# Embedding product of the short tile: both parts of its operand side by side

## The chip, the cores and the metric

The kernel runs on one core of one Trainium2 chip. The metric is the device time of one execution in microseconds, as the median of several runs. The profile is taken on one further execution, whose span (first to last instruction) is a little shorter than its device time.

## The reference, cut to what matters

One layer of a streaming encoder trunk is computed for a prompt of 2048 rows and a sample of 32 rows, with 1024 channels. The last step of the layer adds a gated embedding; a final norm closes it:

```python
    h = h + jnp.concatenate([yA, yB], axis=-1) @ w_out
    gate = jax.nn.sigmoid(rmsnorm(h, g_ple) @ w_ple_gate)
    h = h + (p @ w_ple) * gate
    ...
    return rmsnorm(h, g_final)
```

`p` has 256 channels and `w_ple` is 256 x 1024. The product `p @ w_ple` for the 32 sample rows is what the change touches.

## The kernel before

**Precision.** The products' operands are of type fp32r, to which fp32 is rounded. Each operand is therefore split into an upper part (ACT casts it) and a lower part (DVE subtracts the upper from the original, `split`, L77), and a product is the sum of three: upper x upper, upper x lower, lower x upper.

**Rows.** The 2080 rows are 17 tiles: 16 of 128 rows, and tile 16 with the 32 sample rows, the short tile. `tiles[i]` gives first row and number of rows.

**Stages.** The first stage computes the input projection and the mixers in groups of 416 columns (L572) and, as side work, transposes the embedding inputs `p`, splits them and stores them to `pp_d` (`turn_p`, L1155 to L1193), one record of 128 x 512 for each tile: upper and lower part, two chunks of 128 channels, up to 128 rows. The second stage multiplies with `w_out` in pairs of tiles by a scheme of seven half-size products instead of eight (`seven`, L204, products at L161). Then come the embedding products, then the gate stage, in pairs again.

**The embedding product** of a tile (`embed`, L119) loads the record `pps` from `pp_d` (`load_pps`, L113, on POOL's queue here), multiplies it with the two parts of `w_ple` (`wq`) for each half of the columns, `nh`, into one bank of PSUM (`e`), has ACT copy the bank to `eout` (L141) and stores `eout` to `e_d`, from where the gate stage loads it (`e`). One half of the columns takes two chunks times three combinations, six products, whatever the number of rows:

```python
    def embed_product(ps, pps, wp, cs, n=P):
        for k in range(2):
            for q, (a, b) in enumerate(((0, 0), (0, 1), (1, 0))):
                nc.tensor.matmul(ps[:n], pps[:, a, k, :n], wp[k][b][:, cs], ...)
```

Tiles 3 to 14 and 16 are computed this way before the gate stage, tiles 14 and 16 last. Tiles 0 to 2 were done in the first stage, and tile 15 is done inside the last pair (`last_pair`, L1495).

**The gate stage** begins with the short tile (`plain`, L269, whose products are `packed`, L258). There both parts of the rows lie beside each other already: one product with 64 stationary columns (upper and lower part, L264) and one with 32 (L267) take the place of three, the sums of the lower part stand in rows 32 to 63 of the bank, and DVE adds them (`short_ops`, L1477). Then eight pairs of tiles follow. `prep_g` (L1581) makes a pair's operands while the pair before is computed: DVE transposes one tile of `hn` (L1446), ACT copies the other to `ho` (L1433) for eight transposes on PE (`pth`, L1435), and DVE forms sums (`g_fS`, L1592) and the parts of seven operands (L78, L81). A pair's seven products need, in order, the operands 11, 12, S2, S1, S3, S4 and 22. Their sums leave PSUM by ACT copies (`c_g`, L1455) and DVE additions (L1463); a sigmoid on ACT (L1464), a multiplication and an addition on DVE (L1466, L1467) and the final norm follow (`done_g`: row sums on ACT at L91, 1/sqrt on POOL at L70 and L74, scaling on DVE at L1474, and the store on POOL's queue).

**The order.** The kernel is written in Tile: the framework's scheduler sets the order of the instructions on each engine when the program is built, by estimates of its own, except where the kernel pins it. Each engine then runs its instructions strictly in that order, and DMAs stand in the order of the engine that issues them (SP, POOL or ACT). A changed instruction can so change the order of others that come later.

Of the kernel before, what the change touches and what calls it, by code (L numbers as in the profile page):

```python
# [9 lines left out]
F32 = mybir.dt.float32  # L10
F32R = mybir.dt.float32r
AF = mybir.ActivationFunctionType
ALU = mybir.AluOpType
PSUM = bass.MemoryType.PSUM

P = 128
# [6 lines left out]
PLE = 256  # L23
# [11 lines left out]
def trunk(ctx, tc, x_p, x_s, c_conv, c_pool, p_p, p_s, g_mix, w_in, conv_w, conv_b, pool_w,  # L35
          pool_scale, w_out, g_ple, w_gate, w_ple, g_fin, y_p, y_s, sc_p, sp_p, sc_s, sp_s):
    nc = tc.nc
# [9 lines left out]
    pp_d = tc.dram_tile([NT, P, 2 * PLE], F32, name="pp_d")  # L47
# [5 lines left out]
    def bank(name):  # L53
        return ps_m.tile([P, 512], F32, tag="mm", name=name)
# [22 lines left out]
    def split(hi, lo, src, eng=nc.vector, later=False):  # L77
        ins = nc.scalar.copy(hi, src)  # L78
        if later:
            tc.keep_in_program_order(ins)  # L80
        eng.tensor_tensor(lo, src, hi.bitcast(F32), op=ALU.subtract)  # L81
        return ins
# [14 lines left out]
    tiles = [(i * P, P) for i in range(SEQ // P)] + [(SEQ, DEC)]  # L97
# [1 line left out]
    def rows_of(pr, sa, r, n):  # L99
        return pr[r:r + n] if r < SEQ else sa  # L100

    def embed_product(ps, pps, wp, cs, n=P):
        for k in range(2):
            for q, (a, b) in enumerate(((0, 0), (0, 1), (1, 0))):
                nc.tensor.matmul(ps[:n], pps[:, a, k, :n], wp[k][b][:, cs], start=k + q == 0, stop=k == 1 and q == 2)  # L105


    def load_ple(t, k):
# [2 lines left out]
            nc.sync.dma_start(t[q * 32:q * 32 + 32], w_ple[r:r + 32])  # L111

    def load_pps(t, i, queue):  # L113
        n = tiles[i][1]
        queue.dma_start(t.rearrange("p a k n -> p (a k) n")[:, :, :n].bitcast(F32),
                        pp_d[i].rearrange("p (a n) -> p a n", a=4)[:, :, :n])
        return t

    def embed(todo, wp, ring, queue=nc.sync, loads=nc.sync):  # L119

        got = {}

        def prep(c):
            if c not in got and c < len(todo):
                got[c] = load_pps(ring("pps", todo[c]), todo[c], loads)

        def run(c, last=False):  # L130
            i = todo[c]
            r, n = tiles[i]
            for ahead in range(4):
                prep(c + ahead)
            pps = got[c]
            o = ring("out", i)
            for nh in range(2):
                cs = slice(nh * NH, nh * NH + NH)
                ps = bank(f"e_{i}_{nh}")
                embed_product(ps, pps, wp, cs, n)  # L140
                (nc.vector.tensor_copy if last and nh else nc.scalar.copy)(o[:n, cs], ps[:n])  # L141
            (nc.gpsimd if last else queue).dma_start(e_d[r:r + n], o[:n])

        return prep, run
# [141 lines left out]
    def slot(name):  # L286
        return acts[0].tile([P, SLOT], F32R, tag="hn", name=name)
# [13 lines left out]
    def ring4(t, name):  # L301
        return t.tile([P, D], F32, tag="t", name=name)
# [15 lines left out]
    def load_rows(pool, name, i, pr, sa=None, queue=nc.sync):  # L318
        r, n = tiles[i]
        t = ring4(pool, f"{name}_{i}")  # L320
        queue.dma_start(t[:n], pr[r:r + n] if sa is None else rows_of(pr, sa, r, n))
        return t

    with ExitStack() as s1:
# [152 lines left out]
        def staged(name):  # L477
            return xin.tile([P, KH, 2, P], F32R, tag="t", name=name)
# [676 lines left out]
        def turn_p():  # L1155

            def load(a):
                t = ring4(xin, f"p_{a}")
                for q in range(4):
                    part, cs = t[q * 32:q * 32 + 32], slice(q * 64, q * 64 + 64)  # L1160
                    if a < NT - 1:
                        nc.gpsimd.dma_start(part.rearrange("p (m c) -> p m c", c=64),
                                            p_p[a * P:(a + 4) * P, cs].rearrange("(m p) c -> p m c", p=32))
                    else:
                        nc.gpsimd.dma_start(part[:, :64], p_s[:, cs])
                return t

            rounds = [*range(0, NT - 1, 4), NT - 1]
            t = load(0)
            yield  # L1170
            for a, after in zip(rounds, rounds[1:] + [None]):
                w = D if a < NT - 1 else 64
                nc.vector.transpose(t[:, :w], t[:, :w])
                v = t[:, :w]
                if after is not None:
                    t = load(after)
                yield
                for b in range(0, 4 if w == D else 1, 2):
                    s = staged(f"pps_{a + b}").rearrange("p a h n -> p (a h n)")
                    for c in range(2 if w == D else 1):  # L1180
                        i = a + b + c
                        n = tiles[i][1]
                        o = s[:, c * 2 * PLE:(c + 1) * 2 * PLE].rearrange("p (a k n) -> p a k n", a=2, k=2)[:, :, :, :n]
                        if n == P:
                            src = v[:, (b + c) * PLE:(b + c + 1) * PLE].rearrange("p (g k r) -> p k g r", g=4, k=2)
                            hi, lo = (o[:, h].rearrange("p k (g r) -> p k g r", g=4) for h in range(2))
                        else:
                            src = v.rearrange("p (k r) -> p k r", k=2)
                            hi, lo = o[:, 0], o[:, 1]
                        split(hi, lo, src)  # L1190
                        nc.gpsimd.dma_start(pp_d[i].rearrange("p (a n) -> p a n", a=4)[:, :, :n],
                                            o.rearrange("p a k n -> p (a k) n").bitcast(F32))
                    yield  # L1193

        def at_pace(steps, num, den):
# [12 lines left out]
        for gi, tbs in enumerate(GROUPS):  # L1208
            if gi == 2:

                frames_in.close()
                t = slot("hn_4")
# [37 lines left out]
    with ExitStack() as s2:  # L1250
# [113 lines left out]
        for i in range(0, NT - 1, 2):  # L1364
# [6 lines left out]
            if last:  # L1371
                n = tiles[NT - 1][1]
# [13 lines left out]
        def embedding_chunks(name):  # L1386
            wp = []
            for k in range(2):
                raw = ring4(ya, f"{name}r_{k}")
                load_ple(raw, k)  # L1390
                t = [cmb.tile([P, KH, 2, P], F32R, tag="c", name=f"{name}_{k}_{h}").rearrange("p a b c -> p (a b c)")
                     for h in range(2)]
                split(t[0], t[1], raw)
                wp.append(t)
            return wp

        wp = embedding_chunks("wq")
# [3 lines left out]
        def ring(what, i):  # L1401
            if what == "pps":
                return st.tile([P, 2, 2, P], F32R, tag="t", name=f"pps_{i}")
            if what == "out" and i not in rest_e[-LATE:]:
                return cmb.tile([P, D], F32, tag="c", name=f"eout_{i}")
            return ring4(ya, f"e{what}_{i}")
# [212 lines left out]
        n = tiles[NT - 1][1]  # L1619
# [6 lines left out]
        h, e = (load_rows(*a) for a in ((xh, "h", NT - 1, h_d), (ya, "e", NT - 1, e_d)))  # L1626
        plain("gl", A, W, n, *short_ops(h, e, n))
        done_g(NT - 1, h)
        for i in range(0, NT - 3, 2):
            A = S.pop(i)  # L1630
            h = [load_rows(xh, "h", i + b, h_d) for b in range(2)]
# [34 lines left out]
```

## Time and profile before

| | |
|---|---|
| runs shown | 927.29, 930.17 and 5190.86 us, median 930.17 |
| profiled execution | 929.13 us, span 927.2 us |
| busy in the span | PE 912.1, DVE 719.7, ACT 483.5, POOL 159.6 us |
| matmuls | 4553 |
| granted TensorE clock | 0.998 |

One run is far outside; the others and the profiled execution lie within 2.9 us. The busy time of PE is the time in which a matmul was under way, and consecutive matmuls overlap, so the time that one costs is read from start to start. A row of the timeline has the start in the span, the duration, engine, line, operation, the tile written and the tiles read, the shape and the count; in brackets stands how long the engine had idled before and what ended the idling.

### The profile page before, as it was taken

How to read it: one execution, taken by the hardware profiler on the slowest of the kernel's cores; microseconds unless marked ns; L12 is line 12 of the kernel's file. 1: busy time of each engine (PE TensorE's matmuls, PEld its weight loads, DVE VectorE, ACT ScalarE, POOL GpSimd, SP SyncE). 2: the span in 40 equal slices, each digit the busy share in tenths (PEclk: the TensorE clock that was granted, in tenths of full speed). 3: DMA queues.
4: the chain of work that ended last, by engine and by line, in shares of the span. 5: the costliest groups of instructions: out<-in, count | busy, mean ns of one | idle time of the engine just before them, and what ended most of it. 6: DMA issues, size and time to landing. Idle time of an engine off the chain costs nothing.

```text
span 927.2 us, 13211 instructions
## 1 busy us (share of the span) xinstructions
PE 912.1 (98%) x4553; PEld 826.3 (89%) x4553; DVE 719.7 (78%) x1221; ACT 483.5 (52%) x895; POOL 159.6 (17%) x299
## 2 busy tenths in 40 slices
PE   8999999999999999999999999999999999999996
PEld 6999998999999999999999987888878768888885
DVE  6996989999577869795777678765558658889885
ACT  7743565654345545443544356334336755565563
POOL 3111222121001234110000010111203301111113
PEclk9999999999999999999999999999999999999999
DMA  8357687798936567769655349866787964676663
GB/s 249 98 147 217 168 259 217 230 298 294 410 114 188 173 167 229 187 227 309 184 166 178 122 178 295 266 188 177 227 240 234 377 220 142 227 252 203 200 197 114
DMA packets 135279, 198.58 MB, mean 214 GB/s; under 512 B 12796, under 2 KB 99740, under 8 KB 133933
## 3 DMA queue, kind: packets, MB, share of 16 engines
q1 hardware_dynamic: 115661, 136.65, 47.5%
q0 software_dynamic: 16816, 55.65, 18.8%
q10 hardware_dynamic: 2736, 5.44, 1.8%
q8 instruction: 36, 0.59, 0.3%
q14 instruction: 30, 0.25, 0.1%
HBM read 133.84 MB, written 63.84 MB: 213 GB/s over the span
## 4 chain that ended last, share of the span: by engine, by line
PE 60%; DVE 2%; DMA 2%; issue 1%; ACT 1%; POOL 0%; POOLq 0%; SPq 0%; DVEq 0%; ACTq 0%
PE x_g L161 8%; PE x_o L161 8%; PE z_g L161 4%; PE z_o L161 4%; PE e L105 3%; PE x_zab L572 3%; PE x_ch L572 2%; PE y_g L161 2%; PE x_zbv L572 2%; PE b L572 2%; PE v L572 2%; PE c L572 2%; PE zb L572 2%; PE h L572 2%; PE za L572 2%; PE y_o L161 2%
## 5 line engine op out<-in xcount | busy, mean ns | idle before, releaser
L78 ACT CAST y_S<-y_fS 128x512 fp32r<-128x512 f32 x32 | 19.5, 622 | 40.4 <-PE x_o L161 19.8
L105 PE MATMUL e<-wq,pps 128*128 128x512 f32 (+1 forms) x156 | 36.2, 391 | 0.9 <-DMA pps<-pp_d 0.9
L161 PE MATMUL x_g<-wg_b,g_S 128*128 128x512 f32 x128 | 36.7, 392 | 0.0
L161 PE MATMUL x_o<-wo_b,y_S 128*128 128x512 f32 x128 | 35.8, 391 | 0.0
L105 PEld LDWEIGHTS e<-wq,pps 128*128 128x128 f32 (+1 forms) x156 | 28.2, 182 | 8.2 <-ACT wg_a L78 1.3
L572 PE MATMUL z_ch<-B,w_ch_S 128*128 128x416 f32 x168 | 34.3, 352 | 0.0
L572 PE MATMUL x_zbv<-B,w_zbv_S 128*128 128x416 f32 x168 | 34.2, 352 | 0.0
L572 PE MATMUL z_zbv<-B,w_zbv_S 128*128 128x416 f32 x168 | 34.2, 352 | 0.0
L572 PE MATMUL z_zab<-B,w_zab_S 128*128 128x416 f32 x168 | 34.2, 352 | 0.0
L572 PE MATMUL x_zab<-B,w_zab_S 128*128 128x416 f32 x168 | 34.1, 351 | 0.0
L572 PE MATMUL x_ch<-B,w_ch_S 128*128 128x416 f32 x168 | 34.0, 351 | 0.0
L572 PEld LDWEIGHTS x_ch<-B,w_ch_S 128*128 128x128 f32 x168 | 31.4, 188 | 0.3
L572 PEld LDWEIGHTS x_zab<-B,w_zab_S 128*128 128x128 f32 x168 | 31.3, 188 | 0.3
L572 PEld LDWEIGHTS x_zbv<-B,w_zbv_S 128*128 128x128 f32 x168 | 31.3, 188 | 0.4
L572 PEld LDWEIGHTS z_zab<-B,w_zab_S 128*128 128x128 f32 x168 | 31.3, 188 | 0.3
L572 PEld LDWEIGHTS z_zbv<-B,w_zbv_S 128*128 128x128 f32 x168 | 31.3, 188 | 0.3
L572 PEld LDWEIGHTS z_ch<-B,w_ch_S 128*128 128x128 f32 x168 | 31.3, 188 | 0.3
L78 ACT CAST y<-y 128x512 fp32r<-128x512 f32 x24 | 14.8, 618 | 30.7 <-PE x_o L161 14.4
L406 DVE SCALAR_TENSOR_TENSOR xt<-xt,rstd_x,g_bc 128x1024 f32<-128x1024 f32 (+2 forms) x14 | 17.9, 1282 | 16.2 <-POOL rstd_x L74 16.2
L70 POOL TENSOR_SCALAR ms_f<-ssq_f 128x1 f32<-128x1 f32 (+1 forms) x15 | 7.6, 509 | 131.0 <-ACT junk L91 131.0
L1269 DVE TENSOR_TENSOR c_o<-x_o,x 128x512 f32<-128x512 f32 x14 | 9.7, 690 | 25.1 <-PE x_o L161 25.1
L161 PEld LDWEIGHTS x_o<-wo_b,y_S 128*128 128x128 f32 x128 | 23.9, 188 | 5.6 <-ACT y_S L78 0.4
(584 smaller groups left out, 2697.1 us busy)
## 6 DMA issues: line engine op xcount, KB each, us to landing
y<-y_d SPq DMA_DIRECT2D x16, 512.0 KB, 10.2
x<-in_x_prompt_dram SPq DMA_DIRECT2D x16, 512.0 KB, 6.0
h_d<-x SPq DMA_DIRECT2D x16, 512.0 KB, 4.3
h<-h_d SPq DMA_DIRECT2D x16, 512.0 KB, 3.9
xt<-in_x_prompt_dram SPq DMA_DIRECT2D x15, 512.0 KB, 7.4
e<-e_d SPq DMA_DIRECT2D x15, 512.0 KB, 4.5
out_dram<-h POOLq DMA_DIRECT2D x14, 512.0 KB, 3.1
p_dT<-T POOLq DMA_DIRECT2D x12, 512.0 KB, 6.2
```

Source lines behind the costliest of these rows:

```text
L70: nc.gpsimd.tensor_scalar(ms[:n], ssq[:n], scalar1=1.0 / D, scalar2=EPS, op0=ALU.mult, op1=ALU.add)
L78: ins = nc.scalar.copy(hi, src)
L105: nc.tensor.matmul(ps[:n], pps[:, a, k, :n], wp[k][b][:, cs], start=k + q == 0, stop=k == 1 and q == 2)
L161: nc.tensor.matmul(ps[:n], lhs[:, k, a, :n], w[b][:, k], start=start and k + q == 0, stop=k == KH - 1 and q == 2, skip_group_check=True)
L406: nc.vector.scalar_tensor_tensor(xt[:n], xt[:n], r[:n], g_bc[:n], op0=ALU.mult, op1=ALU.mult)
L572: nc.tensor.matmul(ps[:, :NB], lhs[:, k, x], b[:, k, y], start=start and k + q == 0, stop=stop and k == KH - 1 and q == 2, skip_group_chec ...
L1269: add = lambda o, a, b: nc.vector.tensor_tensor(o, a, b, op=ALU.add)
```

## The change

The short tile's record in `pp_d` is packed: for each of the two chunks, the 32 rows' upper part and then their lower part, 128 numbers in one piece a partition, in place of four pieces of 32. Store and load move that one piece. The product of the short tile takes both parts of a chunk as one stationary operand of 64 columns against the upper part of the weights, and the upper part alone (32 columns) against the lower part of the weights. Rows 0 to 31 of the bank then hold upper x upper plus upper x lower, rows 32 to 63 hold lower x upper. ACT copies the first group to `eout`, and DVE adds the second group onto it. The records of 128 rows keep their layout, and their products stay as they are.

```diff
-    def embed_product(ps, pps, wp, cs, n=P):
+    def embed_product(ps, pps, wp, cs):
         for k in range(2):
             for q, (a, b) in enumerate(((0, 0), (0, 1), (1, 0))):
-                nc.tensor.matmul(ps[:n], pps[:, a, k, :n], wp[k][b][:, cs], start=k + q == 0, stop=k == 1 and q == 2)
+                nc.tensor.matmul(ps, pps[:, a, k], wp[k][b][:, cs], start=k + q == 0, stop=k == 1 and q == 2)
...
     def load_pps(t, i, queue):
-        n = tiles[i][1]
-        queue.dma_start(t.rearrange("p a k n -> p (a k) n")[:, :, :n].bitcast(F32),
-                        pp_d[i].rearrange("p (a n) -> p a n", a=4)[:, :, :n])
+        n = 4 * tiles[i][1]
+        queue.dma_start(t.rearrange("p a k n -> p (a k n)")[:, :n].bitcast(F32), pp_d[i, :, :n])
         return t
+
+    def short_embed_product(ps, pps, wp, cs, n):
+
+        a = pps.rearrange("p a k n -> p (a k n)")[:, :4 * n].rearrange("p (k m) -> p k m", k=2)
+        for k in range(2):
+            for b, m in ((0, 2 * n), (1, n)):
+                nc.tensor.matmul(ps[:m], a[:, k, :m], wp[k][b][:, cs], start=k + b == 0, stop=k + b == 2,
+                                 skip_group_check=True)
...
-                embed_product(ps, pps, wp, cs, n)
+                if n < P:
+                    short_embed_product(ps, pps, wp, cs, n)
+                    nc.scalar.copy(o[:n, cs], ps[:n])
+                    nc.vector.tensor_tensor(o[:n, cs], ps[n:2 * n], o[:n, cs], op=ALU.add)
+                    continue
+                embed_product(ps, pps, wp, cs)
...
-                        o = s[:, c * 2 * PLE:(c + 1) * 2 * PLE].rearrange("p (a k n) -> p a k n", a=2, k=2)[:, :, :, :n]
+                        flat = s[:, c * 2 * PLE:c * 2 * PLE + 4 * n]
                         if n == P:
+                            o = flat.rearrange("p (a k n) -> p a k n", a=2, k=2)
...
-                            hi, lo = o[:, 0], o[:, 1]
+                            hi, lo = (flat.rearrange("p (k a n) -> p a k n", a=2, k=2)[:, h] for h in range(2))
                         split(hi, lo, src)
-                        nc.gpsimd.dma_start(pp_d[i].rearrange("p (a n) -> p a n", a=4)[:, :, :n],
-                                            o.rearrange("p a k n -> p (a k) n").bitcast(F32))
+                        nc.gpsimd.dma_start(pp_d[i, :, :4 * n], flat.bitcast(F32))
```

In the built program, the order of the instructions is the same as before on every engine up to tile 16's products, except for these instructions themselves. After them the scheduler's order differs on all engines: among others, ACT's copy of the first short gate product stands ahead of the copies of tiles 14 and 16, and the eight transposes of most pairs stand later among the products.

## The prediction

> **What bounds the kernel now.** I read the page first: the busy shares and the chain that ended last.
>
> ```profile
> span 927.2 us, 13211 instructions
> PE 912.1 (98%) x4553; PEld 826.3 (89%) x4553; DVE 719.7 (78%) x1221; ACT 483.5 (52%) x895; POOL 159.6 (17%) x299
> PE 60%; DVE 2%; DMA 2%; issue 1%; ACT 1%; POOL 0%; POOLq 0%; SPq 0%; DVEq 0%; ACTq 0%
> ```
>
> TensorE is busy for 98% of the span. The built order of instructions is the same for both kernels up to the products of the short tile (32 rows, tile 16), so only what follows them can change; I then asked what PE waited for from 700 us on, and how full the engines are in one stretch of the gate stage (columns: stretch, PE, PEld, DVE, ACT and POOL busy with counts, clock, DMA share, GB/s).
>
> ```profile
> engine line waited for: us in total, times, longest us
> PE e L105 <- DMA pps<-pp_d: 0.9, 1, 0.9
> PE z_g L161 <- ACT c_g L1455: 0.4, 1, 0.4
> 830.00:850.00 20.00, 20.00 (x96) 16.62 (x95) 18.26 (x27) 11.32 (x20) 3.18 (x6) 1.00 0.67 223
> ```
>
> PE waits twice in 227 us, and the first wait lies before the change. The gate stage is PE bound, but DVE is 91% full: a product taken from PE pays in full, provided that DVE still delivers the operands in time. The place itself, in PE's timeline:
>
> ```profile
> 743.45 5.80 PE L105 MATMUL e<-wq,pps 128*128 128x512 f32 x24
> 749.08 1.08 PE L264 MATMUL x_gl<-wg_c,gl_a 128*64 128x512 f32 x4
> 750.00 1.09 PE L267 MATMUL x_gl<-wg_c,gl_a 128*32 128x512 f32 x4
> 750.93 1.07 PE L264 MATMUL z_gl<-wg_a,gl_a 128*64 128x512 f32 x4
> ...
> 754.61 1.04 PE L1435 MATMUL pth<-ident,ho 128*128 128x128 f32 x8
> 755.40 1.16 PE L264 MATMUL x_gl<-wg_c,gl_a 128*64 128x512 f32 x4
> 756.39 1.09 PE L267 MATMUL x_gl<-wg_d,gl_a 128*32 128x512 f32 x4
> 757.32 2.90 PE L161 MATMUL x_g<-wg_c,g 128*128 128x512 f32 x12
> ```
>
> The 24 are tile 14's and tile 16's twelve products each; the gate products of the short tile follow, then the first pair, without a gap.
>
> **The change, part by part. The products.** Tile 16 has 12 products before, 8 after (per half of the columns: 64, 32, 64, 32 stationary columns). The two evictions of tile 16 each wait for six products:
>
> ```profile
> 747.89 0.57 ACT L141 COPY eout<-e 32x512 f32<-32x512 f32 x1 [0.81 <-PE e L105]
> 749.28 0.57 ACT L141 COPY eout<-e 32x512 f32<-32x512 f32 x1 [0.81 <-PE e L105]
> L264 PEld LDWEIGHTS x_gl<-wg_c,gl_a 128*64 128x64 f32 x8 | 1.1, 135 | 0.6
> L105 PEld LDWEIGHTS e<-wq,pps 128*32 128x32 f32 x12 | 1.3, 109 | 1.4
> ```
>
> They start 1.39 us apart, 0.232 us a product. Products of 64 and of 32 stationary columns run in the short tile's gate already: four of either take 0.92 to 0.93 us (749.08, 750.00, 750.93 above), so the wider operand costs nothing; its weight load (135 ns against 109) fits under a product. Four products less: -4 x 0.232 = **-0.93 us**, all on PE's path. Bounds: if the four went at the pace of the long stages (0.227, last pair below), -0.91; by the step from 743.45 to 749.08 over 24 products (0.235), -0.94.
>
> A rule of the Trainium skill prices a warm product otherwise: "TensorE: Matmul & The Clock Gate", section "Wait — 56ns, not 53.3ns?", has the time from start to start as the moving columns over 2.4 GHz plus some 2.5 ns, 215.7 ns for 512 columns, whatever the stationary width. By that the term would be -0.86 us; the rows have 0.232 and 0.227, so here the trace decides.
>
> **The additions on DVE.** Two new instructions of 32x512 from PSUM, 0.68 us each by the like of it in the gate of the short tile (751.74 below), 0.60 from start to start. DVE idles there before, so their own cost is nothing; the order around them is the question. In the new order ACT copies x_gl (the gate's first product) *ahead* of the four evictions of tiles 14 and 16, so these wait for x_gl; DVE has the x_gl addition, the first new addition, the transpose of hn, the second new addition. The rows before:
>
> ```profile
> 751.13 0.58 ACT L1455 COPY c_gl<-x_gl 32x512 f32<-32x512 f32 x1 [1.27 <-PE x_gl L267]
> 751.61 1.14 ACT L1433 COPY ho<-hn 128x512 f32<-128x512 f32 x2
> 755.25 1.07 ACT L78 CAST g<-pth 128x512 fp32r<-128x512 f32 x2 [2.50 <-PE pth L1435]
> 747.09 1.25 DVE L1446 STREAM_TRANSPOSE hn<-hn 128x1024 f32<-128x1024 f32 x1 [2.87 <-DMA hn<-h_d]
> 751.74 0.68 DVE L1483 TENSOR_TENSOR c_gl<-x_gl,c_gl 32x512 f32<-32x512 f32 x1 [3.40 <-ACT c_gl L1455]
> 756.13 0.67 DVE L81 TENSOR_TENSOR g<-pth,g 128x512 fp32r<-128x512 f32 x1
> 756.73 0.67 DVE L1592 TENSOR_TENSOR g_fS<-g_fS,pth 128x512 f32<-128x512 f32 x1
> ```
>
> Walked with these: x_gl starts at 749.08 - 0.93 = 748.15, its ACT copy 2.05 later (751.13 - 749.08) at 750.20. Copies follow each other by 0.5: the four evictions until 752.7, the two ho copies until 753.8. The new order has PE transpose ho one group of four products later, which after the gain is again 754.6: 0.8 us to spare. DVE: x_gl addition at 750.8, first new addition 752.3 (its eviction ends 752.25), transpose 752.9 to 754.1, second addition 754.15, the sum g_fS 754.75, a z_gl addition 755.35, then the lower part of the first pair's first operand 755.95 to 756.6. The product that reads it is the third of the first pair: 757.32 - 0.93 + 2 x 0.227 = 756.84. It is in time by 0.2 us, and its upper part (ACT, 755.25 + 0.62 = 755.9) by 0.5. So **0** for this part, between 0 and +0.9 (all given back, if ACT and DVE run 1.1 us later than walked).
>
> SP is held too: the store of tile 16's sum waits for the second addition (754.8 instead of ACT's 749.9), and behind it in SP's queue stand the loads of e for tiles 16, 0 and 1 and of hn for the next pair. Median times to landing:
>
> ```profile
> e<-e_d SPq DMA_DIRECT2D x15, 512.0 KB, 4.5
> hn<-h_d SPq DMA_DIRECT2D x28, 128.0 KB, 2.9
> ```
>
> With some 3 us for the store (the smaller of the two sizes) the loads go out from 757.8 on, 5 us later than before, and have landed by 763 (e) and 764 (hn). DVE reads e behind the addition of the first pair's y_g, whose product ends at 756.39 + 2 x 2.72 = 761.8, by the walk at 764; it reads hn behind the fifth product, after 770. Cost 0; if a load came after its reader, DVE's 9% of spare time is the cover.
>
> **The layout of pps** is packed, so the store and the load of tile 16 move the same 64 KB in 128 pieces instead of 512. The load is issued on POOL 8 us before its first reader:
>
> ```profile
> 737.77 0.78 POOL L115 DMA_DIRECT2D pps<-pp_d  x1 [2.18 <-PE e L105]
> DMA to landing us min/median/max: 2.5/4.8/7.6
> ```
>
> It lands before 746 either way; the store and the split lie 350 us earlier, under PE. Cost 0, bounds 0 and, were the landing at the maximum of 7.6 us before and the minimum after, still 0 (743.45 + 12 x 0.235 = 746.3 is when it is read; 737.77 + 7.6 = 745.4).
>
> **The order in the seven pairs after it.** The transposes of the next pair move from the fifth product of seven (x_g of S3, most pairs before) into the sixth (z_g of S4, after four to eleven of its twelve), once into the seventh. I walked the fullest case, four products into z_g. One product of twelve takes 2.72 us (last pair: 905.34 to 908.06), so from the transposes' end to the next pair's first product there are 8 x 0.227 + 2.72 = 4.53 us. ACT's upper part (0.62) follows the first half of the transposes, DVE starts on the lower part 4.0 us ahead of the first product and has it 3.3 us ahead. DVE's next 15 operations follow at 0.60 (756.13 to 756.73 above), while the operands are due 2.72 us apart. Cost 0 while the slip is under 3.3 us.
>
> **The last pair's wait.** Before, PE stood still once:
>
> ```profile
> 900.49 1.06 ACT L91 ACTIVATE junk<-h 128x1024 bf16<-128x1024 f32 x1
> 902.91 1.28 DVE L1474 SCALAR_TENSOR_TENSOR h<-h,rstd_f,g_bc 128x1024 f32<-128x1024 f32 x1 [0.46 <-POOL rstd_f L74]
> 904.83 0.72 ACT L1561 ACTIVATE c_g<-c_g,rs_h 128x512 f32<-128x512 f32 x1 [1.05 <-DVE c_g L1559]
> 908.25 0.63 ACT L1529 ACTIVATE junk<-h 128x512 bf16<-128x512 f32 x1 [1.18 <-DVE h L1521]
> 908.88 0.56 ACT L1455 COPY c_g<-z_g 128x512 f32<-128x512 f32 x1
> 905.34 2.88 PE L161 MATMUL z_g<-wg_a,g_S 128*128 128x512 f32 x12
> 908.06 1.07 PE L161 MATMUL x_g<-wg_b,g_S 128*128 128x512 f32 x4
> 909.50 3.03 PE L161 MATMUL z_g<-wg_d,g_S 128*128 128x512 f32 x12 [0.38 <-ACT c_g L1455]
> ```
>
> The copy of z_g stood behind a sum of squares that waited for DVE; PE went on at 909.50 instead of 908.06 + 4 x 0.227 = 908.97, 0.53 late. In the new order the copy stands ahead of that, behind the sigmoid of the first quarter, which waits for an addition that DVE now does after *both* normalisations of the pair before. Counted from the last pair's first product: the 16 operations from -4.0 on end at 5.6 with tile 13's h, tile 12's being complete at 5.0; the normalisation follows the start of the squares by 2.42 (900.49 to 902.91), so 7.5 to 8.7, the second 8.7 to 9.9, the addition 10.6, the sigmoid 11.3, the copy 11.9. PE wants it at 4 x 2.72 + 4 x 0.227 = 11.8. A wait of 0.1 takes the place of 0.53: **-0.4 us**. Bounds: -0.53 (no wait) to +0.7 (the normalisations 1.2 us, one operation, later). I take the walked value.
>
> **Sum** against the profiled execution: 929.13 (span 927.2 and 1.9 around it) - 0.93 - 0.4 = **927.8 us**. The runs shown have their median at 930.17 (927.29, 930.17 and one far outlier), so the profiled one lies 1.0 under that median and 1.8 above the fastest.
>
> **The rivals.** *Given back in the short tile* (0.22): ACT's and DVE's new order there takes over 1.1 us more than walked and the last pair keeps its wait; for it, the margin of 0.2 us; against it, ACT idle 2.5 us ahead of the cast at 755.25. Then 929.13 - 0.93 + 0.93 = 929.1.
>
> *Slower by the later transposes* (0.12): DVE is 91% full and the operands of each pair are now made after a later point. It decides where the lower part of a pair's first operand comes over 3.3 us later than walked, by a late hn load or by DVE's queue; PE then waits once a pair. One us over in five pairs: 929.13 - 0.93 + 5 = 933.2. Against it: the first pairs have the transposes in z_g before too, and PE does not wait there:
>
> ```profile
> 771.40 0.60 PE L1435 MATMUL pth<-ident,ho 128*128 128x128 f32 x4
> ```
>
>
> *It does not do what it says* (0.06): a pair of 64 and 32 columns into the same rows of PSUM costs more than the rows of the gate's short tile, 0.35 a product instead of 0.232: 8 x 0.35 = 2.8, no gain: 929.13 - 0.4 = 928.7.
>
> **How the numbers follow.** The forecast has 0.60, the rivals the 0.40. From run to run the kernel strays by -1.8 to +1.0 of the profiled time, more than the whole effect. Low: 927.8 - 1.8, and 0.8 for a last wait gone and a run as low again: 925.2. High: the given-back case with the scatter (930.1) and a third of the slower one: 931.2. A change of 2% is 18.6 us, about what a measurement of this kernel can tell from no change; no case reaches it, so 0.01 faster, 0.97 within, 0.02 slower.
>
> **What would show it.** Right: 4,549 products on PE; the 13.9 us from tile 14's first product (743.45) to the first pair's (757.32) become 12.9, without a wait at x_g; PE's wait list from 700 us on shows the z_g wait at 0.1 or gone; the tail after the last product is as long as before. Wrong: a wait of PE for ACT g or DVE g at 756.4, or for ho at the transposes (given back); a wait per pair for pth's operands (slower); more than 1.9 us for the eight products.

## The result, and the profile after

The changed kernel is slower by about two thousandths, where the prediction had it faster by one and a half.

| | median of the runs | profiled execution | its span | mean granted clock |
|---|---|---|---|---|
| before | 928.57 us (21 runs on the chip of the comparison) | 929.13 us | 927.2 us | 0.998 |
| after | 930.48 us (21 runs, 928.03 to 933.57) | 932.43 us | 930.6 us | 0.995 |

The ratio after to before is **1.0024, 95% interval 1.0016 to 1.0031**: 1.5 to 2.9 us. Lines of the kernel after lie 12 higher than those of before (the z and x products of a pair at L173, the copies of `carry` at L1467); the short tile's embedding products have line L123.

The page's head and engine shares, and behind them PE's list of waits from 700 us on:

```profile
span 930.6 us, 13195 instructions
PE 911.9 (98%) x4549; PEld 826.2 (89%) x4549; DVE 720.9 (77%) x1223; ACT 483.6 (52%) x895; POOL 160.5 (17%) x299
```

```profile
engine line waited for: us in total, times, longest us
PE z_g L173 <- ACT c_g L1467: 2.1, 1, 2.1
```

4,549 products, as meant, and one wait: the one of the last pair at z_g, 0.4 us before, 2.1 now. PE's timeline at the place of the change:

```profile
743.89 3.02 PE L105 MATMUL e<-wq,pps 128*128 128x512 f32 x12
746.74 2.01 PE L123 MATMUL e<-wq,pps 128*64 128x512 f32 x8
748.60 1.07 PE L276 MATMUL x_gl<-wg_c,gl_a 128*64 128x512 f32 x4
756.84 2.90 PE L173 MATMUL x_g<-wg_c,g 128*128 128x512 f32 x12
```

The eight products take 748.60 - 746.74 = 1.86 us, 0.232 each. From tile 14's first product to the first pair's there are 12.95 us instead of 13.87: the change takes its 0.92 us out of PE's path, and no wait stands in the short tile. Now the last pair, PE's timeline (the first three rows answer to the last three of the prediction's rows of before) and the clock in stretches of half a microsecond (last three columns: PEclk, DMA share, GB/s):

```profile
904.62 2.88 PE L173 MATMUL z_g<-wg_a,g_S 128*128 128x512 f32 x12
907.35 1.07 PE L173 MATMUL x_g<-wg_b,g_S 128*128 128x512 f32 x4
910.49 4.60 PE L173 MATMUL z_g<-wg_d,g_S 128*128 128x512 f32 x12 [2.07 <-ACT c_g L1467]
914.93 2.01 PE L173 MATMUL x_g<-wg_b,g_S 128*128 128x512 f32 x8
```

```profile
911.00:911.50 0.50, 0.50 (x3) 0.39 (x3) 0.49 (x2) 0.38 (x1) 0.00 (x0) 0.94 1.07 311
911.50:912.00 0.50, 0.50 (x3) 0.34 (x2) 0.50 (x1) 0.42 (x1) 0.45 (x1) 0.50 0.48 131
914.00:914.50 0.50, 0.50 (x2) 0.37 (x2) 0.00 (x0) 0.00 (x0) 0.10 (x1) 0.50 0.00 0
914.50:915.00 0.50, 0.50 (x3) 0.40 (x2) 0.00 (x0) 0.00 (x0) 0.00 (x0) 0.64 0.00 0
```

z_g goes on at 910.49 instead of 907.35 + 0.907 = 908.26: 2.23 us late, against 0.53 before, so +1.70. Then its twelve products take 914.93 - 910.49 = 4.44 us instead of some 2.85, because the granted clock is 0.50 from 911.44 (0.94 over the first half microsecond shown) to 914.86 (0.64 over the last): another +1.6 in this execution. The chain that made the copy of z_g late, from the timelines of DVE, POOL and ACT:

```profile
893.15 0.69 DVE L1478 TENSOR_TENSOR e<-e,c_g 128x512 f32<-128x512 f32 x1 [0.79 <-ACT c_g L1476]
893.76 0.68 DVE L81 TENSOR_TENSOR g<-pth,g 128x512 fp32r<-128x512 f32 x1
902.17 1.29 DVE L1479 TENSOR_TENSOR h<-h,e 128x512 f32<-128x512 f32 x2
904.27 0.37 POOL L70 TENSOR_SCALAR ms_f<-ssq_f 128x1 f32<-128x1 f32 x1 [13.50 <-ACT junk L91]
905.32 1.28 DVE L1486 SCALAR_TENSOR_TENSOR h<-h,rstd_f,g_bc 128x1024 f32<-128x1024 f32 x1 [0.73 <-POOL rstd_f L74]
905.49 1.16 POOL L70 TENSOR_SCALAR ms_f<-ssq_f 128x1 f32<-128x1 f32 x1 [0.21 <-ACT junk L91]
906.73 0.55 POOL L74 TENSOR_TENSOR rstd_f<-ms_f,nhalf 128x1 f32<-128x1 f32 x1
907.32 1.28 DVE L1486 SCALAR_TENSOR_TENSOR h<-h,rstd_f,g_bc 128x1024 f32<-128x1024 f32 x1 [0.72 <-POOL rstd_f L74]
908.52 0.68 DVE L1571 TENSOR_TENSOR c_g<-y_g,c_g 128x512 f32<-128x512 f32 x1
909.24 0.72 ACT L1573 ACTIVATE c_g<-c_g,rs_h 128x512 f32<-128x512 f32 x1 [3.36 <-DVE c_g L1571]
909.87 0.57 ACT L1467 COPY c_g<-z_g 128x512 f32<-128x512 f32 x1
```

Read it from the end: ACT's copy stands behind a sigmoid, the sigmoid waits for DVE's addition of y_g, and that stands behind two normalisations which DVE starts 2.0 us apart, because each waits for GpSimd's statistics (1.16 us for the second `ms_f`, 0.55 for the power). And the two h additions ahead of all this come late. DVE starts on the lower part of the last pair's first operand at 893.76, only 2.71 us ahead of that pair's first product (896.47): work for the pair before stands in front of it, an addition (891.67), ACT's sigmoid that waits for that (892.39), and the multiplication that waits 0.79 us for the sigmoid (893.15). The lateness shows further back too: DVE's transpose for the last pair stands at 887.34 before and at 889.79 after, 18.0 and 14.8 us ahead of the z_g products of S1 at 905.34 and 904.62. First before, then after:

```profile
887.34 1.24 DVE L1446 STREAM_TRANSPOSE hn<-hn 128x1024 f32<-128x1024 f32 x1
```

```profile
889.79 1.24 DVE L1458 STREAM_TRANSPOSE hn<-hn 128x1024 f32<-128x1024 f32 x1
```

One more thing lies behind the last product: the last piece of the output (in the list of DMA issues of the tail, us to landing) takes 3.5 us instead of 2.7, before and after:

```profile
out_dram<-hg ACTq DMA_DIRECT2D x1, 192.0 KB, 2.7
```

```profile
out_dram<-hg ACTq DMA_DIRECT2D x1, 192.0 KB, 3.5
```

The balance of the two profiled executions, 932.43 - 929.13 = +3.3: products -0.92, the longer wait +1.70, the low clock +1.6, the last piece +0.8, a short tile that starts 0.44 later for reasons ahead of the change, and -0.3 that is left over.

### The profile page after: what moved, and what is told of

The parts are those of the page before. It is cut to its first block, busy times and chain, and to the rows that moved or that the text cites. A ratio compares the mean times of both kernels' runs of the same rounds, so it can differ in the third digit from the quotient of the medians.

```text
span 930.6 us, 13195 instructions
## 1 busy us (share of the span) xinstructions
PE 911.9 (98%) x4549; PEld 826.2 (89%) x4549; DVE 720.9 (77%) x1223; ACT 483.6 (52%) x895; POOL 160.5 (17%) x299
## 5 line engine op out<-in xcount | busy, mean ns | idle before, releaser
L173 PE MATMUL x_g<-wg_b,g_S 128*128 128x512 f32 x128 | 35.7, 389 | 0.0
L173 PE MATMUL x_o<-wo_b,y_S 128*128 128x512 f32 x128 | 35.7, 390 | 0.0
L105 PE MATMUL e<-wq,pps 128*128 128x512 f32 x144 | 33.5, 391 | 0.0
L105 PEld LDWEIGHTS e<-wq,pps 128*128 128x128 f32 x144 | 26.8, 188 | 6.2 <-ACT eout L153 0.7
L1486 DVE SCALAR_TENSOR_TENSOR h<-h,rstd_f,g_bc 128x1024 f32<-128x1024 f32 (+1 forms) x15 | 19.3, 1284 | 13.7 <-POOL rstd_f L74 13.7
```

Source lines behind the costliest of these rows:

```text
L105: nc.tensor.matmul(ps, pps[:, a, k], wp[k][b][:, cs], start=k + q == 0, stop=k == 1 and q == 2)
L173: nc.tensor.matmul(ps[:n], lhs[:, k, a, :n], w[b][:, k], start=start and k + q == 0, stop=k == KH - 1 and q == 2, skip_group_check=True)
L1486: nc.vector.scalar_tensor_tensor(h[:n], h[:n], rf[:n], g_bc[:n], op0=ALU.mult, op1=ALU.mult)
```

## The experiments

Theory after the result: two additions in the short tile turn the order in which the scheduler places DVE's and ACT's work behind them; the loss is a wait in the last pair, made of late DVE work *and* a late place of the y addition, with what follows that wait. Rivals: the loss lies in the short tile, in every pair, or in the last transfer. The table has the wait of PE at z_g in the last pair from each profile; the ratios are to the kernel before on the same chip.

| kernel | ratio, 95% interval | wait at z_g, us | largest other wait of PE in the gate stage, us | last piece, us |
|---|---|---|---|---|
| after, again | 1.0033, 1.0020 to 1.0047 | 2.06 | none | 3.5 |
| y addition first | 1.0003, 0.9994 to 1.0012 | none | 1.39, last x_g | 3.5 |
| z copy first | 1.0006, 0.9993 to 1.0019 | none | 0.91, last x_g | 3.5 |
| idle filled | 1.0021, 1.0010 to 1.0033 | none | none | 3.5 |
| before, late order | 1.0002, 0.9991 to 1.0012 | none | none | 2.7 |
| without the additions | 0.9993, 0.9982 to 1.0003 | none | none | 2.7 |
| additions as written | 1.0096, 1.0080 to 1.0111 | 0.21 | 5.55, transposes | 2.7 |
| the same, two orders | 1.0103, 1.0079 to 1.0126 | none | 6.0, transposes | 2.7 |
| two orders | 1.0005, 0.9994 to 1.0016 | none | none | 3.5 |
| before, two orders | 1.0010, 1.0001 to 1.0019 | 0.40 | none | 2.7 |
| additions early | 1.0002, 0.9989 to 1.0014 | 0.82 | 0.24, first x_g | 3.5 |
| additions early, two orders | 0.9988, 0.9975 to 1.0001 | none | 0.24, first x_g | 2.7 |

**The changed kernel again.** No edit.

> The changed kernel itself once more, on the chip of the three others. If its loss is the wait at z_g (2.2 us of idle against 0.5) and, in some of its runs, a stretch of low clock after it: ratio 1.0015 to 1.003, with a mean granted clock of 0.995 or 0.996 in about half of the runs and 0.997 or 0.998 in the others, the former slower by 1 to 1.6 us in the median. If the loss was that one chip's or that set's scatter: ratio 1.000.

Measured: 1.0033, the loss is there on a second chip. Its profile shows the same wait *without* the low clock:

```profile
908.46 1.07 PE L173 MATMUL x_g<-wg_b,g_S 128*128 128x512 f32 x4
911.59 3.01 PE L173 MATMUL z_g<-wg_d,g_S 128*128 128x512 f32 x12 [2.06 <-ACT c_g L1467]
914.44 1.75 PE L173 MATMUL x_g<-wg_b,g_S 128*128 128x512 f32 x7
```

```profile
913.00:915.00 2.00, 2.00 (x11) 1.65 (x10) 1.10 (x2) 0.41 (x2) 1.91 (x2) 1.00 0.55 209
```

Here z_g's products take 2.85 us at a clock of 1.00. So the wait is a property of the kernel, and the low clock comes in a part of its executions only. The split by mean clock that I expected did not hold: 0.995 stood in 5 of 11 runs, with a median of 931.9 us against 931.1 for the others, among them the two slowest runs (the profiled one had its low clock at 16 to 20 us and not at the wait). In the 21 runs of the result it does hold: ten have 0.995, with a median of 930.9 us against 929.7. How often the low clock falls at the wait is left open by this, since a mean does not say where the clock was low.

**The y addition ahead of the normalisations**, in the last pair on DVE; the normalisations of tiles 12 and 13 are handed to `last_pair` as `scaled`.

```diff
-            nc.vector.scalar_tensor_tensor(h[:n], h[:n], rf[:n], g_bc[:n], ...)
+            def scaled():
+                nc.vector.scalar_tensor_tensor(h[:n], h[:n], rf[:n], g_bc[:n], ...)
...
-                    tt(c, ps, c, op=ALU.add)
+                    ins = tt(c, ps, c, op=ALU.add)
+                    if at == (0, 0):
+                        with tc.issue_after(ins.ins):
+                            for rest in scaled: rest()
```

> The changed kernel with one order written by hand: in the last pair, DVE adds the y product to the first carried sum ahead of the two normalisations of tiles 12 and 13, not behind them. Theory (order of the last pair): ACT's sigmoid no longer waits for GpSimd's statistics, the copy of z_g runs as soon as its product is there, TensorE's idle of 2.2 us at about 908 us is gone (0.3 us or less left), and with it the stretch in which the granted clock was 0.50 to 0.81, which cost 1.6 us. Time 3.8 us below the changed kernel: about 926.7 us, ratio to the kernel before 0.998. Rival (loss spread over the short tile, the seven pairs and the last transfer): the wait goes but the time stays at 930 us or loses only the 1.7 us of the wait that is new, ratio 1.000 to 1.002.

```profile
907.07 2.94 PE L173 MATMUL z_g<-wg_d,g_S 128*128 128x512 f32 x12
914.57 3.06 PE L173 MATMUL x_g<-wg_T,g 128*128 128x512 f32 x12 [1.39 <-DVE c_g L1577]
```

The wait and the low clock are gone, as the theory has it, with DVE's transposes as late as in the changed kernel; but 1.39 us of the gain went into a new wait further on, for the addition that frees the bank of x_g. The ratio fell from 1.0024 to 1.0003, not to the 0.998 that was expected; the last piece of the output, 0.8 us later than in the kernel before, stays as well.

**The z copy ahead of the sigmoid** of the first quarter (held back in `held` with what follows it), on ACT; DVE's order stays.

```diff
+            def carry(ps, at):
+                if at != (1, 1): return copied(ps, at)
+                t = st.tile([P, NH], F32, tag="t", name="c_z")
+                with tc.issue_after(nc.scalar.copy(t, ps).ins):
+                    held.pop()()
+                return t
```

> The changed kernel with another order written by hand: on ACT, the copy of z_g stands ahead of the sigmoid of the first quarter of the last pair; DVE's order stays. Theory (order of the last pair): the copy runs at about 907.6 to 908.2, TensorE waits at most 0.1 us, the granted clock stays at 1.00, the time falls by 3.8 us to about 926.7 us (ratio 0.998), although the sigmoid and all that DVE does for tile 14 come no earlier than in the changed kernel. If tile 14's own chain were what the end waits for, the time would stay above 929 us. Rival (loss spread elsewhere): 930 us, ratio 1.002.

```profile
906.12 2.95 PE L173 MATMUL z_g<-wg_d,g_S 128*128 128x512 f32 x12
913.15 3.01 PE L173 MATMUL x_g<-wg_T,g 128*128 128x512 f32 x12 [0.91 <-DVE c_z L1581]
```

The same from the other side: no wait at z_g, 0.91 us of a new one. Two edits that have nothing in common but that wait bring the time back to that of before; that the loss as a whole is in the short tile or in the pairs is out.

**The idle filled** with ten products into a bank that is overwritten later, so that nothing else moves.

```diff
+            def fill():
+                ps = bank("e_l1_0")
+                for k in range(10):
+                    nc.tensor.matmul(ps, pps[:, 0, 0], wp[0][0][:, NH:], start=True, stop=True)
```

> The changed kernel with ten products more (128x512, into the bank that the last embedding product overwrites later) between the four x_g products and z_g of the last pair, 2.27 us of work by the 0.227 us of its rows, where TensorE idled for 2.2 us; every other instruction keeps its order, so z_g starts as late as in the changed kernel. Theory (the idle lowers the granted clock, and that costs 1.6 us beside the wait): clock 1.00 all through, z_g's twelve products take 2.9 us and not 4.4, time 1.6 us below the changed kernel, about 928.9 us, ratio 1.0005. Rival (the low clock after the wait is a mark in the records and costs nothing, or comes from something else than the idle): z_g still takes 4.4 us, time 930.5 us, ratio 1.002.

```profile
911.15 2.43 PE L1593 MATMUL e_l<-wl,pps_l 128*128 128x512 f32 x10
913.42 2.99 PE L173 MATMUL z_g<-wg_d,g_S 128*128 128x512 f32 x12
916.25 1.98 PE L264 MATMUL x_g<-wg_b,g_S 128*128 128x512 f32 x8
```

In the profile z_g's products take 2.83 us, as expected; the time did not fall. What the low clock costs where it comes can be read from one fixed point ahead of the change, the eight small transposes before tile 14's products, to the issue of the last store: 182.93 us in the first profile of the changed kernel (743.28 to 926.21), 181.37 in the second (744.32 to 925.69), where the clock stayed up at the wait without any filling, and 181.38 here (746.11 to 927.49). So it cost that one execution 1.56 us. Its mean cost is open: the runs here, seven of them with an interval of 0.0023, can't tell it from nothing.

**The kernel before with the late order** in its last pair: the y addition behind both normalisations, the z copy behind the sigmoid.

```diff
+                    with tc.issue_after(scaled[1].ins):
+                        tt(c, ps, c, op=ALU.add)
...
+                    with tc.issue_after(held.pop().ins):
+                        return copied(ps, at)
```

> The kernel before (twelve products in the short tile) with the changed kernel's order of the last pair written by hand: DVE adds the y product behind both normalisations, and ACT copies z_g behind the sigmoid of the first quarter. Theory (order of the last pair): TensorE waits 1.5 to 2.2 us at z_g where it waited 0.4, the granted clock falls below 0.9 after it, and the time rises by 2 to 3.3 us to 930.6 to 931.9 us, ratio 1.002 to 1.0035, with no change to the products at all. Rival (the loss belongs to the new products and additions): 928.6 us to 930.3 us for the wait alone, ratio 1.000 to 1.0018, clock 1.00.

```profile
905.16 1.28 DVE L1474 SCALAR_TENSOR_TENSOR h<-h,rstd_f,g_bc 128x1024 f32<-128x1024 f32 x1 [1.53 <-POOL rstd_f L74]
906.36 0.69 DVE L1572 TENSOR_TENSOR c_g<-y_g,c_g 128x512 f32<-128x512 f32 x1
907.72 0.57 ACT L1455 COPY c_g<-z_g 128x512 f32<-128x512 f32 x1
908.39 2.97 PE L161 MATMUL z_g<-wg_d,g_S 128*128 128x512 f32 x12
```

The theory as I had it falls: the late order alone makes no wait. The z_g products of S1 start at 904.76 here; the y addition comes 1.60 us behind that, in the changed kernel 908.52 - 904.62 = 3.90. With the runs that follow, this says that the order costs only where DVE's work for the pair before is late as well.

**Without the two additions.** Products and layout as changed.

```diff
                     short_embed_product(ps, pps, wp, cs, n)
                     nc.scalar.copy(o[:n, cs], ps[:n])
-                    nc.vector.tensor_tensor(o[:n, cs], ps[n:2 * n], o[:n, cs], op=ALU.add)
```

> The changed kernel without DVE's two additions in the short tile: its embedding rows lack the products of the lower parts with the upper parts of the weights, everything else is computed. The eight products and the packed layout stay. Theory (the products are worth 0.9 us, the additions only turn the order): the order of the last pair is nearly that of the kernel before, TensorE waits 0.5 us or less there, and the time falls by 0.7 to 1.4 us, ratio 0.9985 to 0.9993. Rival (the products are not worth 0.9 us, something in the short tile gives it back): ratio 1.000 or above although no wait shows in the last pair.

```profile
906.75 1.52 PE L172 MATMUL x_g<-wg_b,g_S 128*128 128x512 f32 x6
908.11 2.88 PE L172 MATMUL z_g<-wg_d,g_S 128*128 128x512 f32 x12
```

With the additions gone, the scheduler's order in the pairs is nearly that of before, and z_g follows without a wait. 0.9993 is -0.65 us, interval -1.7 to +0.3: about what the products should bring, though no change is inside the interval too. It isn't the products alone. PE's last twelve products start 1.8 us sooner, counted from the same fixed point, for the old wait is gone as well; but from their start to the issue of the last store it takes 6.04 us instead of 5.33.

**The additions held where they are written.**

```diff
-                    nc.scalar.copy(o[:n, cs], ps[:n])
-                    nc.vector.tensor_tensor(o[:n, cs], ps[n:2 * n], o[:n, cs], op=ALU.add)
+                    tc.keep_in_program_order(nc.scalar.copy(o[:n, cs], ps[:n]))
+                    tc.keep_in_program_order(nc.vector.tensor_tensor(o[:n, cs], ps[n:2 * n], o[:n, cs], op=ALU.add))
```

> The changed kernel with the short tile's two copies and two additions held in the order in which they are written. By that alone the scheduler places DVE's stream transpose in the later pairs ahead of the second normalisation again, as in the kernel before, while in the last pair the y product is still added behind both normalisations. Theory as the runs so far mend it (both are needed: the pairs' DVE work late by about 3 us, and the addition behind the normalisations): the normalisations end 2 to 3 us earlier against the last pair's products, TensorE waits 0.3 us or less at z_g, the clock stays at 1.00, ratio 0.999 to 1.0005. Rival (the order behind the normalisations alone makes the wait): TensorE waits 1.5 us or more at z_g, ratio 1.001 to 1.0025.

```profile
751.10 13.24 SPq L154 DMA_DIRECT2D e_d<-eout  x2
762.72 1.28 DVE L150 TENSOR_TENSOR eout<-e,eout 32x512 f32<-32x512 f32 x2
781.50 1.97 PE L1447 MATMUL pth<-ident,ho 128*128 128x128 f32 x8 [5.55 <-ACT ho L1445]
917.65 3.02 PE L173 MATMUL z_g<-wg_d,g_S 128*128 128x512 f32 x12 [0.21 <-ACT c_g L1467]
```

A miss with two answers in it. DVE makes the additions only at 762.72 (752.68 and 754.45 in the changed kernel), so the store of tile 16's sum holds SP's queue until 764.3 and the loads of e and hn behind it are late; DVE, which is nearly full, stands 3.63 us for e and falls behind, and PE stands 5.55 us at the transposes of the next pair: this is how the short tile can make the kernel slow, and additions some 9 to 10 us later than in the changed kernel are enough. The last pair, though, answers what was asked: with early transposes (19.7 us ahead of the S1 products, 18.0 in the kernel before) and the y addition behind both normalisations the wait at z_g is 0.21 us. That rest is not the y addition's, which starts 0.27 us ahead of the S1 products; ACT's copy stands behind a sum of squares here. The order on DVE is not the one that was expected: the transpose stands behind both normalisations of a pair here (888.62, 890.63, 893.92), as it does in the kernel before and in the changed one; what is early is its place against PE's products. PE's stall may have its part in that, so this run shows the wait that goes with it, and not what the order alone does. The same with both orders of the last pair set by hand:

> The changed kernel with three orders written by hand: the short tile's copies and additions as written, in the last pair the y product added ahead of both normalisations, and the x product's addition directly behind the z product's (in the kernel with the y addition first, TensorE waited 1.4 us for it before its last twelve x products). Theory: no wait of TensorE over 0.3 us from the short tile to its last product, clock 1.00 up to there; 0.93 us from the products and 0.4 us from the old wait are kept: 1.3 us below the kernel before, ratio 0.9986, bounds 0.998 to 0.9995. Rival (every reorder only moves the wait on, or the last tile's own chain ends last): ratio 1.000 or above.

It met the same stall (6.0 us), and none in the last pair; ratio 1.0103.

**Two orders in the last pair**: the y addition first, and the x addition directly behind the z addition; on the changed kernel, and on the kernel before.

```diff
+                if at == (0, 1):
+                    held.append(lambda: finish(b, half, ...))
+                elif at == (1, 1):
+                    with tc.issue_after(ins.ins):
+                        held.pop()()
```

> The changed kernel with the order of its last pair written by hand at two places: DVE adds the y product ahead of both normalisations, and the x product directly behind the z product. Short tile and other pairs as in the changed kernel, the late transposes too. Theory: no wait at z_g, and the wait of 1.4 us before the last twelve x products, which came with the first order alone, falls to 0.2 us or less; what is left is the products' 0.93 us and the old wait of 0.4 us: ratio 0.9986, bounds 0.998 to 0.9998. Rival (a third wait comes, or the short tile and the pairs give the gain back): ratio 1.000 or above.

> The kernel before with the same two orders by hand and its twelve products. Theory: its wait of 0.4 us at z_g goes, nothing else changes: ratio 0.9996, bounds 0.999 to 1.0005; the changed kernel with the same orders lies 0.9 us (0.001) below it, which is the products' worth. Rival (the products are worth nothing): both kernels of this call have the same ratio.

The changed kernel has no wait left in the gate stage, yet its ratio is 1.0005, the rival's number. The gain is given back behind PE's last products:

```profile
915.56 1.59 PE L105 MATMUL e_l<-wl,pps_l 128*128 128x256 f32 x12
916.49 0.62 ACT L1570 ACTIVATE hg<-hg,rstd_l 128x384 f32<-128x384 f32 x1 [1.45 <-POOL rstd_l L1564]
922.07 0.38 ACTq L1571 DMA_DIRECT2D out_dram<-hg  x1
```

From the start of PE's last twelve products to the issue of the last store it takes 6.51 us, in the kernel before 5.33. The last quarter's sigmoid on ACT stands behind a scaling that waits for GpSimd; the scaling starts 0.93 us behind the start of those products, in the kernel before 0.50 us ahead of it (917.78 and 918.28). After that the last piece lands in 3.5 us instead of 2.7. The kernel before with the two orders pays at the first place too, 6.05 us, which fits its ratio above 1; and it keeps its 0.40 us at z_g, for on ACT a sum of squares that waits for DVE stands ahead of the copy, so the theory's word on it was wrong. 1.0005 and 1.0010 lie within each other's intervals, so the times don't resolve the products' 0.9 us. PE's timeline does: from the fixed point to PE's last twelve products it is 175.48 us in the kernel before with the two orders, 173.97 in the changed kernel with them, 1.51 less, of which 0.92 is the products and some 0.5 the wait at z_g.

**The additions early**: the gate's work on ACT and DVE held behind them.

```diff
+        with tc.issue_after(added[0].ins), tc.issue_after(added[1].ins):
             plain("gl", A, W, n, *short_ops(h, e, n))
```

> The changed kernel with one order held: ACT's and DVE's work for the short tile's gate stands behind the two evictions and additions of its embedding, so the additions come right behind their products, where the kernel before has the evictions. Everything is computed. The pairs' transposes stand nearly where they stood in the kernel before; in the last pair the y product is still added behind both normalisations. Theory (late transposes and late addition are both needed for the long wait): TensorE waits 0.6 us or less at z_g, clock 1.00 there, and with the 0.93 us of the products the ratio is 0.9985 to 1.0000. Rival (the late addition alone is enough): wait of 1.5 us or more, ratio 1.001 or above. Second rival (the additions in the short tile cost TensorE what the products bring): a wait of TensorE between 745 and 760 us.

```profile
907.51 3.01 PE L175 MATMUL z_g<-wg_d,g_S 128*128 128x512 f32 x12 [0.82 <-ACT c_g L1469]
```

With the additions where the evictions were, the wait is 0.82 us instead of 2.1, a little above what I expected, and the ratio 1.0002, above the range that was expected too. The transpose stands 15.8 us ahead of the S1 products here, and the y addition 2.64 us behind their start.

**Early additions and both orders**, the version to which the runs point.

> The same with the two orders in the last pair as well: the y product added ahead of both normalisations, the x product directly behind the z product. Theory: no wait of TensorE over 0.3 us from the short tile to its last product; 0.93 us from the products and 0.4 us of the old wait: ratio 0.9986 where the last piece of the output lands in 2.7 us as in the kernel before, 0.9994 where it takes 3.5 us as in the changed kernel. Rival (a reorder always moves the wait on): a wait of 0.8 us or more at another place, ratio 1.000 or above.

```profile
754.84 0.50 PE L175 MATMUL x_g<-wg_c,g 128*128 128x512 f32 x1 [0.24 <-ACT g L78]
908.14 2.95 PE L175 MATMUL z_g<-wg_d,g_S 128*128 128x512 f32 x12
914.10 2.88 PE L175 MATMUL x_g<-wg_T,g 128*128 128x512 f32 x12
```

One wait of 0.24 us is left behind the short tile, none in the last pair; the tail from PE's last twelve products to the issue of the last store keeps 5.96 us. 0.9988, interval 0.9975 to 1.0001, median 927.89 us against 928.70. It lies below the changed kernel (whose intervals begin at 1.0016 and 1.0020) with the same products and the same sums, by order alone, and has the lowest ratio of all kernels here; that it beats the kernel before is likely, and just not shown by the interval.

## Why the prediction was wrong

- **The products, -0.93 us: right.** 1.86 us for eight, 12.95 us where there were 13.87. The rival that the packed product doesn't do what it says (2.8 us for eight) is out.
- **The additions and the short tile, 0: right.** No wait there; the lower part of the first pair's first operand starts 0.37 us later than walked, less than the 0.44 us by which the short tile itself starts later. The rival "given back in the short tile" is out. Its price was set too low, though: the kernel with the additions some 9 to 10 us later lost 0.0096.
- **The later transposes, 0: wrong in what it left out.** No pair waits for its operands, as argued. But the step asked only whether the *next* operands are in time. What DVE does with the rest of the pair (the two h additions that feed the normalisations) is pushed back as well, and this slip is carried into the last pair. With the y addition behind both normalisations, the wait at z_g is 0 (before with the late order) or 0.21 us (additions as written) where the transposes are 18.0 or 19.7 us ahead of the S1 products, 0.82 where it is 15.8 (additions early), and 2.1 where it is 14.8 (after).
- **The last pair's wait: the step that failed.** Walked -0.4 with bounds of -0.53 and +0.7; measured +1.70. Counted from the last pair's first product (896.47) both h additions end at 7.0 where the walk had 5.6 for the later one. The sixteen operations took what the walk gave them (9.7 us for 9.6), but they began at -2.7 and not at -4.0: the walk let ACT and DVE start as soon as PE's transposes gave them something, and both had work for the pair before ahead of that, ACT the sigmoid and DVE the multiplication that waits for it. The normalisations were set to follow each other by one operation, at 7.5 and 8.7; they start at 8.85 and 10.85, since ACT's second sum of squares comes 1.2 us behind the first (GpSimd starts on them, `ms_f`, at 904.27 and 905.49) and GpSimd then takes 1.16 us for the second `ms_f` where it took 0.37 for the first: the spacing is that of ACT and GpSimd, not DVE's. Together 2.07 us on the copy, whose end was walked at 11.9 and is at 13.97. The upper bound allowed for one operation late; two things were late, the start by 1.3 us and the second normalisation by 0.8 more.
- **What the sum didn't have:** the low clock behind a wait (+1.6 us in one profiled execution of two), and the last piece of output (+0.8, see the last section).
- The mechanism was named in the right place, with the right queue behind it (the copy behind the sigmoid behind the addition behind both normalisations). Taken with 2.2 us of wait the prediction's own sum would have been 929.13 - 0.93 + 1.7 = 929.9, slower than before.

## What to carry to other kernels

Where a scheduler decides the order, a small edit is paid for where it moves others, and that may be 150 us later: follow the *whole* queue of the fullest engine to the end of the stage, not only the operands that PE reads next. Two instructions that each wait for a third engine don't follow each other by their own length; take the spacing from the slowest link of their chain. And a margin of 0.1 us at the end of a walk of sixteen operations is no forecast of the sign: the bound should have held two late links, which would have brought the slower side into it. And time taken from the fullest engine counts only as far as the tail behind its last instruction lets it: read that tail before and after as well.

## What was unexpected of the hardware

**The clock.** After 2.07 us of idle by the profile (2.23 by the pace of the products, 908.26 to 910.49) PE ran at a granted clock of 0.50 for some 3.4 us in one execution, and after 2.06 us by the profile at the same place it kept 1.00 in another. Waits of 1.39 and 0.91 us left it at 1.00; the 5.55 us of the kernel with the additions as written brought it down, and there it was at 0.50 from 778 us on, 2 us after PE fell idle at 775.95. The Trainium skill, "TensorE: Matmul & The Clock Gate", section "Part 1: The HAM clock gate", has a free-running window of about 3.4 us and the half clock after at least one idle window. The length of the low stretch and its coming and going fit such a window; that a whole idle window is needed does not, for about 2 us were enough here, and the measurement decides.

**The last piece of output.** In seven of the fourteen profiles it landed in 2.7 us, in the other seven in 3.5, the same for the changed kernel on both chips. The piece is 192 KB in all of them. What parts the two groups is a load of 8 KB of instructions (DMA queue q14, one packet): in the seven of 3.5 us it starts 1.9 us behind the issue of the last store, while that store's packets are under way; in the seven of 2.7 it comes either before the store's first packet or more than 4 us behind the issue, after the landing. Six packets of the last two stores take 0.18 to 0.21 us in each of the profiles with 3.5, and none over 0.13 in the others. The first of them start 0.7 us ahead of the load, so how the one delays the other is not shown, and no run moved the load alone. That the 0.8 us go with the program, and not with the execution, fits it.
